# A decoder layer's first feed-forward product: three of eight pairs of tiles by seven products in eight of ten groups

## The chip, the cores and the metric

One core of one Trainium2 chip runs the whole kernel. The metric is device microseconds (us) of one execution; lower is better. Engines are named as in the profile: PE is TensorE's matmul row and PEld its weight loads, DVE is VectorE, ACT is ScalarE, POOL is GpSimd, SP is SyncE, whose queue issues the DMAs.

## The reference

One layer of a decoder for 256 tokens of width 2048 in float32: a token mixer (four mLSTM heads and eight dilated-attention heads), cross-attention into 256 memory tokens, and a SwiGLU channel mixer, each followed by `x <- LN(alpha * x + f(x))`. The change lies in the channel mixer:

```
def swiglu_ffn(x, w1, w3, w2):
    return (jax.nn.silu(x @ w1) * (x @ w3)) @ w2
```

with `x` 256 x 2048, `w1` and `w3` 2048 x 5632 and `w2` 5632 x 2048.

## The kernel before

**Numbers.** Every float32 operand is split into a high part (ACT casts it, L114) and a low part (DVE subtracts the high part from the operand, L115). A product is three matmuls, high by high, high by low and low by high, added up in PSUM.

**Groups and blocks.** The first feed-forward product is made in eleven groups of hidden features, `f0`, `f2`, ... `f20`; `f0` has code of its own, the ten others run in the loop at the end of `decoder_layer`. One group multiplies x2 (the layer's input at that point, 256 x 2048) by 1024 weight columns, 512 of `w1` and `w3` each. It walks over eight blocks of weights. A block is two 128-row tiles (a pair) by 1024 columns, 1 MB, fetched by SP in two DMAs of 512 KB (`fetch_pair`, L210) into one of RAW = 3 buffers, named `f18w` in group f18. The DMA for a block waits until DVE has read the last of the block that lay in that buffer.

**Plain blocks.** `plain` splits the two tiles (two casts and two subtractions of 128 x 1024) into `f18h` and `f18l`; there are SPLIT = 5 buffers for each. `tile_products` then issues 24 matmuls of 128 x 512 columns: 2 tiles x 2 token halves x 2 column halves x 3.

**Blocks by seven products.** A block in parentheses in `plan`, such as `(2,)`, is taken as a 2 x 2 product of quarter blocks, with seven products in place of eight, the Strassen-Winograd scheme: 21 matmuls. Three DVE instructions form the sums of weights: L292 (128 x 1024, into `f18t`), L296 and L297 (128 x 512 each, into `f18s`). Then four pieces are split, of 512, 1024, 1024 and 1024 columns. I call them P1, P23, P57 and Q64 after the products they serve; block 2's are 2.P23 and so on, and the two halves of a plain block 7 are 7a and 7b. The matching sums of x2 (`x2m`) are made once, by `mix_again`, and kept.

**Banks.** P2, P3, Q4 and E gather the plain blocks too. After the last block by seven, `early` (L679 to L683) empties the banks P1, P5, P7 and Q6 on DVE while plain blocks still run; `whole` (L691) adds the other four when the group ends. `hidden` then applies silu and the gate, transposes and splits the result into `hT`, and for the pairs listed in SEVENS also mixes it (L145 to L148, `hTm`). That work falls into the next group's time.

**What sets the order.** All of this part is ordered by the framework: it replays the program on a cost model of its own while it lays instructions out, so the order on each engine is fixed when the kernel is built, and so is the choice of buffers. At run time each engine takes its instructions in that order and waits on semaphores. An L292 that waits for its block's DMA therefore holds all that stands behind it on DVE.

The ten groups used `plan = [0, 1, (2,), 3, 4, (5,), 6, 7]`. In groups f2 and f4, DVE also applies the norm's gain and bias to z (`ln.rest`, L745), one instruction after each block. After f10, the first half of the second feed-forward product (`w2a0`, `w2a1`) runs, after f20 the rest (`w2b0`, `w2b1`).

**Memory.** On-chip working memory beside the pools is cut into NSLOT slots of 128 x 1024 float32 (4,096 bytes of each partition), handed out in turn by `big` and, in halves, `slot`.

Of the kernel before, what the change touches and what calls it, by code (L numbers as in the profile page):

```python
# [11 lines left out]
F32 = mybir.dt.float32  # L12
F32R = mybir.dt.float32r
# [6 lines left out]
P = 128  # L20
D = 2048
S = 256
KT = D // P
# [9 lines left out]
NEG = -1.0e30  # L33
U = 2 * S - 1
W = 1024
NSLOT, RAW, SPLIT = 34, 3, 5
LAG, HEAD, POOLED, LAG2 = 6, 8, 5, 8
WARM = 2

# [13 lines left out]
def decoder_layer(ctx: ExitStack, tc: tile.TileContext, A):  # L53
# [4 lines left out]
    const = ctx.enter_context(tc.tile_pool(name="const", bufs=1))  # L58
# [12 lines left out]
    def big(name, dt=F32R):  # L71
        i = free_slots.pop(0)
        t = up.tile([P, 1024], dt, tag=f"u{i}", name=name)
        held[id(t)] = (i, t)
        return t

    def slot(name):
        if len(free_halves) < 3 and free_slots:
            t = big(name, F32)
            i, _ = held.pop(id(t))  # L80
            pair = {"i": i, "free": 2}
            for c in range(2):
                free_halves.append((t[:, c * 512 : (c + 1) * 512], pair))
        t, pair = free_halves.pop(0)
        pair["free"] -= 1
        held[id(t)] = (pair, t)
        return t

    def free(*tiles):
        for t in tiles:  # L90
            where, _ = held.pop(id(t))
            if isinstance(where, int):
                free_slots.append(where)
                continue
            where["free"] += 1
            if where["free"] == 2:
                free_halves[:] = [x for x in free_halves if x[1] is not where]
                free_slots.append(where["i"])
            else:
                free_halves.append((t, where))  # L100
# [93 lines left out]
    def fetch(src, name):  # L194


        def get(b):
            w = wp.tile([P, 2, W], F32, tag="w", name=f"{name}w{b}", bufs=RAW)
            nc.sync.dma_start(out=w, in_=src[b])
            return w  # L200

        return get

    def fetch_pair(src, name):


        def get(b):
            w = wp.tile([P, 2, W], F32, tag="w", name=f"{name}w{b}", bufs=RAW)
            for c in range(2):
                nc.sync.dma_start(  # L210
                    out=w[:, :, c * 512 : (c + 1) * 512],
                    in_=src[c][b // 2][:, b % 2].rearrange("p (s c) -> p s c", s=2),
                )
            return w

        return get
# [454 lines left out]
    def into_rows(rows, name):  # L671


        def early(of):
            u = slot(f"{name}u")
            for m in range(2):
                rows.append([slot(f"{name}{m}{c}") for c in range(2)])
            (r11, r12), (r21, r22) = rows
            SC.copy(r11, of["P1"])  # L679
            V.tensor_tensor(out=u, in0=r11, in1=of["Q6"], op=ALU.subtract)  # L680
            V.tensor_tensor(out=r21, in0=u, in1=of["P7"], op=ALU.add)
            V.tensor_tensor(out=r12, in0=of["P5"], in1=u, op=ALU.subtract)
            V.tensor_tensor(out=r22, in0=r12, in1=of["P7"], op=ALU.subtract)  # L683
            free(u)

        return early

    def whole(rows, banks):
        for m in range(2):
            for c in range(2):  # L690
                V.tensor_tensor(out=rows[m][c], in0=rows[m][c], in1=banks[m][c], op=ALU.add)  # L691
# [100 lines left out]
    sel_t = slot("sel")  # L792
# [3 lines left out]
    nc.sync.dma_start(out=cw, in_=A["conv"])  # L796
    gb = const.tile([8, 1], F32, tag="gb", name="gb")
    nc.sync.dma_start(out=gb, in_=A["gate_b"])
    gw = const.tile([P, KT, 8], F32, tag="gw", name="gw")
    nc.sync.dma_start(out=gw, in_=A["w_gate"])  # L800

    gw2 = const.tile([P, KT, 40], F32R, tag="gw2", name="gw2")
    gz = slot("gwz")
    V.memset(gz, 0.0)
    V.tensor_copy(gw2[:, :, 8:32], gz.rearrange("p (k c) -> p k c", k=KT)[:, :, :24])
# [6 lines left out]
        attention(2 * j, qk0[j], qk0[2 + j], [va[m][0] for m in range(2)], tb)  # L812
    qk1 = in_features(2) + in_features(3)
    es, least_norm = gates()
    free(sel_t)
    for j in range(2):
        attention(4 + 2 * j, qk1[j], qk1[2 + j], [va[m][1] for m in range(2)], tb)
    free(*va[0], *va[1])
# [63 lines left out]
    for g in range(2):  # L882
        get, plan = fetch(A["w_out"][g], f"wo{g}"), [0, 2, (1,), 4, 5, (3,), 6, 7]
# [101 lines left out]
    plan = [0, 2, (1,), 4, (3,), 5, 6, 7]  # L985
# [3 lines left out]
    plan, kept = [0, (1,), 2, (3,), 4, 5, 6, 7], range(KT - LAG, KT)  # L989
# [115 lines left out]
    def hidden(j, banks, parts, name):  # L1105

        for i in range(2):
            hs = []
            for m in range(2):
                h = slot(f"{name}h{i}{m}")  # L1110
                g, u = parts(banks[m], i)
                SC.activation(h[:, :256], g, ACT.Silu)
                V.tensor_tensor(out=h[:, :256], in0=h[:, :256], in1=u, op=ALU.mult)
                hs.append(h)
            pt = sbank(f"{name}p{i}")
            for s in range(2):
                for m in range(2):
                    T.transpose(
                        pt[:, s * S + m * P : s * S + (m + 1) * P], hs[m][:, s * P : (s + 1) * P], ident
                    )  # L1120
            if j + i in SEVENS:
                h = slot(f"{name}t{i}")
                SC.copy(h, pt)
                hT.put(j + i, h)
                hT.mix(j + i, h)
                free(h)
            else:
                hT.put(j + i, pt)
            free(*hs)
# [4 lines left out]
    def w2_first():  # L1134
        plan = [0, 1, 3, (2,), 5, (4,), 7, (6,), 9, (8,), 10, 11]
        for c in range(2):
            banks = gemm_seven(
                hT, fetch(A["w2"][c][:half], f"w2a{c}"), 2 * half, f"w2a{c}", plan, into_z(c, ALPHA),
                last=c == 1,
            )  # L1140
            for m in range(2):
                add(m, c, banks, scale=1.0)

    for j in (2, 5):
        x2.mix_again(j)
    rest = ln.rest()
    for g in range(2, n, 2):
        get, rows = fetch_pair(A["w13"][g - 2 : g], f"f{g}"), []
        plan = [0, 1, (2,), 3, 4, (5,), 6, 7]
        between = (lambda: next(rest, None)) if g < half else None  # L1150
        banks = gemm_seven(x2, get, KT, f"f{g}", plan, into_rows(rows, f"f{g}r"), last=g == n - 2, between=between)
        whole(rows, banks)
        hidden(g, rows, lambda b, i: [b[i][:, x * 256 : (x + 1) * 256] for x in range(2)], f"f{g}")
        free(*rows[0], *rows[1])
        if g == half - 2:
            w2_first()
# [3 lines left out]
    plan = [0, (1,), 2, (3,), 4, (5,), 6, 7, 8, 9]  # L1160
# [3 lines left out]
    plan = [(1,), 0, (3,), 2, (5,), 4, 6, 7, 8, 9]  # L1164
# [107 lines left out]
```

## Time and profile before

| | us |
|---|---|
| runs of the kernel before | 1541.36, 1539.50, 1541.11 (median 1541.11) |
| the profiled execution | 1540.81 |
| its span, first to last instruction | 1539.0 |
| granted TensorE clock (mean) | 0.998 |

The profile shows one execution, whose own time is 1540.81 us; 1.8 us of that lie outside the span. Rows of the timeline give start, duration, engine, line, operation, out<-in and shape, and in brackets how long the engine had been idle and what ended that. A displayed duration on DVE and PE runs on into the next instruction of the same engine, so what an instruction costs its engine is the distance between two starts when nothing waits. Group f18 lies at 1335.8 to 1378.9 us.

### The profile page before, as it was taken

To read this page: it belongs to the slowest core of one execution; us is meant where nothing else is said; L and a number is where in the kernel's file an instruction comes from. 1 tells how busy PE (TensorE), PEld (TensorE's weight loads), DVE (VectorE), ACT (ScalarE), POOL (GpSimd) and SP (SyncE) were. 2 spreads that over 40 slices of the span, in tenths; PEclk is the share of its full clock that TensorE was granted. 3 is DMA by queue.
4 is the path that set the end of the run, shared out by engine and by line. 5 is a ranking of instruction groups with operands and counts; after the bars stand their busy time and mean duration, and the time that the engine had idled before them with its cause. 6 is when DMAs were issued, how large, how long until landed. Compare 5 with 4: busy or idle time off the path is not lost.

```text
span 1539.0 us, 19369 instructions
## 1 busy us (share of the span) xinstructions
PE 1522.7 (99%) x7394; PEld 1273.8 (83%) x7394; DVE 1233.4 (80%) x1663; ACT 797.0 (52%) x1054; POOL 9.3 (1%) x18
## 2 busy tenths in 40 slices
PE   9999999999999999999999999999999999999997
PEld 7888888888888878888888888887788888888885
DVE  7665788787799888657798788888788878888897
ACT  5444645554544555445557454555545455455551
POOL 0000000000000000000000000000000000000000
PEclk9999999999999999999999999999999999999999
DMA  8674445664654546445564555665455666567552
GB/s 303 208 272 165 140 172 210 232 237 160 232 191 172 205 171 221 162 165 179 177 218 165 174 182 192 218 195 200 156 215 208 200 192 194 192 205 260 197 186 109
DMA packets 83419, 301.37 MB, mean 196 GB/s; under 512 B 7213, under 2 KB 9466, under 8 KB 59774
## 3 DMA queue, kind: packets, MB, share of 16 engines
q1 hardware_dynamic: 83326, 300.14, 56.6%
q8 instruction: 58, 0.95, 0.2%
q14 instruction: 35, 0.29, 0.1%
HBM read 297.99 MB, written 4.21 MB: 196 GB/s over the span
## 4 chain that ended last, share of the span: by engine, by line
PE 95%; DVE 3%; DMA 1%; issue 0%; ACT 0%; DVEq 0%; SPq 0%; ACTq 0%
PE w2a1P L323 2%; PE w2a0P L323 2%; PE w2b0P L323 2%; PE w2b1P L323 2%; PE f10P L323 2%; PE v1P L323 2%; PE xo0P L323 2%; PE wo0P L323 2%; PE f4P L323 2%; PE f14P L323 2%; PE f6P L323 2%; PE f20P L323 2%; PE f16P L323 2%; PE f18P L323 2%; PE v0P L323 2%; PE wo1P L323 2%
## 5 line engine op out<-in xcount | busy, mean ns | idle before, releaser
L114 ACT CAST w2a1h<-w2a1w 128x1024 fp32r<-128x1024 f32 (+1 forms) x24 | 22.5, 980 | 23.3 <-PE w2a1E L323 14.5
L114 ACT CAST w2a0h<-w2a0w 128x1024 fp32r<-128x1024 f32 (+1 forms) x24 | 22.8, 980 | 17.8 <-PE w2a0E L323 10.7
L115 DVE TENSOR_TENSOR w2a0l<-w2a0w,w2a0h 128x1024 fp32r<-128x1024 f32 (+1 forms) x24 | 26.5, 1129 | 6.1 <-ACT w2a0h L114 6.1
L115 DVE TENSOR_TENSOR w2a1l<-w2a1w,w2a1h 128x1024 fp32r<-128x1024 f32 (+1 forms) x24 | 26.3, 1128 | 5.6 <-ACT w2a1h L114 5.6
L114 ACT CAST w2b0h<-w2b0w 128x1024 fp32r<-128x1024 f32 (+1 forms) x20 | 19.3, 987 | 17.3 <-PE w2b0E L323 9.8
L114 ACT CAST w2b1h<-w2b1w 128x512 fp32r<-128x512 f32 (+1 forms) x28 | 19.8, 758 | 12.9 <-PE w2b0E L323 5.4
L323 PE MATMUL w2a0P<-w2a0h,hT 128*128 128x512 f32 x80 | 26.2, 391 | 0.2 <-ACT w2a0h L114 0.2
L323 PE MATMUL w2a1P<-w2a1h,hT 128*128 128x512 f32 x80 | 25.4, 389 | 0.0
L114 ACT CAST wo1h<-wo1w 128x1024 fp32r<-128x1024 f32 (+1 forms) x16 | 15.6, 1001 | 18.9 <-PE wo1E L323 11.3
L264 PE MATMUL f0b<-f0h,x 128*128 128x512 f32 x64 | 25.4, 397 | 0.0
L114 ACT CAST f12h<-f12w 128x1024 fp32r<-128x1024 f32 (+1 forms) x16 | 15.6, 1000 | 18.7 <-PE f12E L323 9.9
L265 PE MATMUL f0b<-f0l,x 128*128 128x512 f32 x64 | 25.1, 392 | 0.1
L114 ACT CAST xv0h<-xv0w 128x1024 fp32r<-128x1024 f32 (+1 forms) x16 | 15.2, 970 | 18.5 <-PE xv0E L323 7.1
L115 DVE TENSOR_TENSOR w2b0l<-w2b0w,w2b0h 128x1024 fp32r<-128x1024 f32 (+1 forms) x20 | 22.2, 1137 | 3.0 <-ACT w2b0h L114 3.0
L115 DVE TENSOR_TENSOR v0l<-v0w,v0h 128x1024 fp32r<-128x1024 f32 (+1 forms) x16 | 18.2, 1154 | 7.8 <-ACT v0h L114 7.7
L115 DVE TENSOR_TENSOR xo0l<-xo0w,xo0h 128x1024 fp32r<-128x1024 f32 (+1 forms) x16 | 18.2, 1153 | 7.3 <-ACT xo0h L114 7.2
L114 ACT CAST v0h<-v0w 128x1024 fp32r<-128x1024 f32 (+1 forms) x16 | 15.7, 1000 | 16.0 <-PE v0E L323 9.9
L114 ACT CAST v2h<-v2w 128x1024 fp32r<-128x1024 f32 (+1 forms) x16 | 15.6, 1000 | 16.2 <-PE v2E L323 10.8
L115 DVE TENSOR_TENSOR w2b1l<-w2b1w,w2b1h 128x512 fp32r<-128x512 f32 (+1 forms) x28 | 22.7, 854 | 1.5 <-ACT w2b1h L114 1.5
L387 PE MATMUL i0b<-xT,i0h 128*128 128x512 f32 x64 | 22.6, 427 | 0.8 <-ACT i0h L114 0.8
L115 DVE TENSOR_TENSOR wo0l<-wo0w,wo0h 128x1024 fp32r<-128x1024 f32 (+1 forms) x16 | 18.2, 1153 | 6.4 <-ACT wo0h L114 6.4
L387 PE MATMUL xk1b<-mT,xk1h 128*128 128x512 f32 x64 | 23.0, 401 | 0.3 <-ACT xk1h L114 0.3
(1719 smaller groups left out, 5556.6 us busy)
## 6 DMA issues: line engine op xcount, KB each, us to landing
w2a0w<-in_w SPq DMA_DIRECT2D x12, 1024.0 KB, 4.8
w2a1w<-in_w SPq DMA_DIRECT2D x12, 1024.0 KB, 5.7
w2b0w<-in_w SPq DMA_DIRECT2D x10, 1024.0 KB, 4.9
w2b1w<-in_w SPq DMA_DIRECT2D x10, 1024.0 KB, 5.0
v0w<-in_w_v SPq DMA_DIRECT2D x8, 1024.0 KB, 5.1
v1w<-in_w_v SPq DMA_DIRECT2D x8, 1024.0 KB, 4.8
v2w<-in_w_v SPq DMA_DIRECT2D x8, 1024.0 KB, 4.8
wo0w<-in_w_out SPq DMA_DIRECT2D x8, 1024.0 KB, 4.9
```

The source lines that it names most:

```text
L114: SC.copy(hi, src)
L115: latest["lo"] = V.tensor_tensor(out=lo, in0=src, in1=as_f32(hi), op=ALU.subtract).ins
L264: T.matmul(banks[m][c], xh, wh[:, cs], start=n == 0, stop=False)
L265: T.matmul(banks[m][c], xh, wl[:, cs], start=False, stop=False)
L323: T.matmul(of[to], lhsT, rhs, start=to not in begun, stop=end)
L387: T.matmul(banks[f], wh[:, cs], op.both(kt), start=kt == 0, stop=end, skip_group_check=True)
```

## The change

The eight groups f6 to f20 take three blocks by seven products, (2,), (4,) and (6,), in place of two, (2,) and (5,), and in another order. Groups f2 and f4 keep two, now (2,) and (4,), in the order 0, 1, 3, (2,), 5, (4,), 6, 7. x2 is mixed for the pairs 2, 4 and 6 in place of 2 and 5; the third kept `x2m` needs a slot, so NSLOT is 35, and the two gate weights `gw` and `gw2`, which had memory of their own for the whole program, live in slots until the gates are made.

```
-NSLOT, RAW, SPLIT = 34, 3, 5
+NSLOT, RAW, SPLIT = 35, 3, 5
...
-    gw = const.tile([P, KT, 8], F32, tag="gw", name="gw")
+    gw_t, gw2_t = slot("gw"), big("gw2")
+    gw = gw_t[:, : KT * 8].rearrange("p (k c) -> p k c", k=KT)
...
-    gw2 = const.tile([P, KT, 40], F32R, tag="gw2", name="gw2")
+    gw2 = gw2_t[:, : KT * 40].rearrange("p (k c) -> p k c", k=KT)
...
-    free(sel_t)
+    free(sel_t, gw_t, gw2_t)
...
-    for j in (2, 5):
+    for j in (2, 4, 6):
         x2.mix_again(j)
...
-        plan = [0, 1, (2,), 3, 4, (5,), 6, 7]
+        plan = [0, 1, 3, (2,), 5, (4,), 6, 7] if g < 6 else [0, 1, (2,), 3, (4,), 5, (6,), 7]
```

One line is added ahead of L800, so L1113 of before is L1114 in the change.

DVE at the end of group f16, before, from the second half of block 7 of f16 (`f16l_11286`) to the second L691; `f18l` are the subtractions of f18's blocks 0 and 1, L292 is the first sum of its block (2,):

```order
L115 TENSOR_TENSOR f16l_11286<-f16w_11266,f16h_11285 128x1024
L681 TENSOR_TENSOR f16ru<-f14t_10973,f16P_10991 128x512
L682 TENSOR_TENSOR f16ru<-f16P_10990,f14t_10973 128x512
L115 TENSOR_TENSOR f18l_11351<-f18w_11347,f18h_11350 128x1024
L683 TENSOR_TENSOR f16r_11224<-f16ru,f16P_10991 128x512
L115 TENSOR_TENSOR f18l_11367<-f18w_11347,f18h_11366 128x1024
L292 TENSOR_TENSOR f18t_11420<-f18w_11417 128x1024
L115 TENSOR_TENSOR f18l_11386<-f18w_11382,f18h_11385 128x1024
L296 TENSOR_TENSOR f18s_11421<-f18t_11420,f18w_11417 128x512
L691 TENSOR_TENSOR f14t_10973<-f14t_10973,f16P_10985 128x512
```

The same place in the change, from `f16l_11350`, the second half of block 7:

```order
L115 TENSOR_TENSOR f16l_11350<-f16w_11330,f16h_11349 128x1024
L115 TENSOR_TENSOR f18l_11415<-f18w_11411,f18h_11414 128x1024
L680 TENSOR_TENSOR f14t_11027<-f14t_11027,f16Q_11046 128x512
L115 TENSOR_TENSOR f18l_11431<-f18w_11411,f18h_11430 128x1024
L115 TENSOR_TENSOR f18l_11450<-f18w_11446,f18h_11449 128x1024
L681 TENSOR_TENSOR f16ru<-f14t_11027,f16P_11045 128x512
L682 TENSOR_TENSOR f16ru<-f16P_11044,f14t_11027 128x512
L292 TENSOR_TENSOR f18t_11484<-f18w_11481 128x1024
L115 TENSOR_TENSOR f18l_11466<-f18w_11446,f18h_11465 128x1024
L691 TENSOR_TENSOR f14t_11027<-f14t_11027,f16P_11039 128x512
```

L292 has moved behind a third subtraction (three of the four halves of blocks 0 and 1 now stand ahead of it), and `early` begins (L680) behind the last subtraction of its group rather than ahead of it.

DVE in the middle of group f18, before, around its second and last L292 (of block (5,)); `f18l_11482` is the second half of block 3, `f18l_11501` and `f18l_11517` are block 4:

```order
L115 TENSOR_TENSOR f18l_11482<-f18w_11462,f18h_11481 128x1024
L292 TENSOR_TENSOR f18t_11535<-f18w_11532 128x1024
L115 TENSOR_TENSOR f18l_11501<-f18w_11497,f18h_11500 128x1024
L145 TENSOR_TENSOR f16h_11317<-f16h_11317 128x128
L146 TENSOR_TENSOR f16h_11317<-f16h_11317 128x128
L115 TENSOR_TENSOR hT_11329<-f16h_11317,hT_11329 128x2x256
L115 TENSOR_TENSOR f18l_11517<-f18w_11497,f18h_11516 128x1024
L296 TENSOR_TENSOR f18s_11536<-f18t_11535,f18w_11532 128x512
```

The same group in the change, around its third L292 (of block (6,)); `f18l_11577`, `f18l_11587` and `f18l_11597` are 4.P23, 4.P57 and 4.Q64, `f18l_11610` is the first half of block 5:

```order
L115 TENSOR_TENSOR f18l_11577<-f18w_11561,f18h_11576 128x1024
L145 TENSOR_TENSOR f16h_11381<-f16h_11381 128x128
L146 TENSOR_TENSOR f16h_11381<-f16h_11381 128x128
L147 TENSOR_TENSOR f16h_11381<-f16h_11381 128x128
L115 TENSOR_TENSOR hT_11393<-f16h_11381,hT_11393 128x2x256
L148 TENSOR_TENSOR f16h_11381<-f16h_11381 128x128
L115 TENSOR_TENSOR f18l_11587<-f18t_11564,f18h_11586 128x1024
L292 TENSOR_TENSOR f18t_11644<-f18w_11641 128x1024
L115 TENSOR_TENSOR f18l_11597<-f18s_11565,f18h_11596 128x1024
L115 TENSOR_TENSOR hTm_11400<-f16h_11381,hTm_11400 128x512
L296 TENSOR_TENSOR f18s_11645<-f18t_11644,f18w_11641 128x512
L115 TENSOR_TENSOR f18l_11610<-f18w_11606,f18h_11609 128x1024
```

L292 of block (6,) now stands in the midst of block (4,)'s splits: 4.Q64 and both halves of block 5 come behind it. The buffer of block (6,)'s weights is the one that block 3 held, so its DMA waits for the second half of block 3 on DVE.

## The prediction

> **What bounds the kernel now.** I read the page first: busy time and the chain of waits.
>
> ```profile
> PE 1522.7 (99%) x7394; PEld 1273.8 (83%) x7394; DVE 1233.4 (80%) x1663; ACT 797.0 (52%) x1054; POOL 9.3 (1%) x18
> PE 95%; DVE 3%; DMA 1%; issue 0%; ACT 0%; DVEq 0%; SPq 0%; ACTq 0%
> ```
>
> PE carries 95% of the chain. A displayed matmul is longer than what it costs, so I checked with the chain's own merged rows and the windows of three groups (columns: window, its length, then busy time and count of PE, PEld, DVE, ACT):
>
> ```profile
> 1336.14 5.44 PE f18P L323 x24
> 1249.50:1292.60 43.10, 43.10 (x195) 35.59 (x194) 34.94 (x46) 23.65 (x29) 0.00 (x0) 1.00 0.60 194
> 1292.60:1335.80 43.20, 43.20 (x196) 35.67 (x195) 36.47 (x46) 23.67 (x29) 0.00 (x0) 1.00 0.61 196
> 1335.80:1378.90 43.10, 43.10 (x196) 35.59 (x195) 34.85 (x46) 23.66 (x29) 0.00 (x0) 1.00 0.62 193
> ```
>
> One matmul costs 5.44 / 24 = 0.2267 us. A group has 6 x 24 + 2 x 21 = 186 of them, 42.17 us; eight small transposes take the other 0.93 of 43.10. Nothing is left for waiting: in these groups PE sets the time. DVE is busy 34.9 to 36.5 us of each 43.1, ACT 23.7. So matmuls taken away shorten the group, as long as DVE keeps up.
>
> **Where a low share of waiting can mislead.** DVE takes its instructions in a fixed order, and an L292 that waits for its weights holds all behind it. The timeline of DVE shows how long such a reload takes: from the start of the subtraction that frees the buffer to the start of the L292 that needs the new weights.
>
> ```profile
> 1258.84 1.22 DVE L115 TENSOR_TENSOR f14l<-f14w,f14h 128x1024 fp32r<-128x1024 f32 x1 [2.60 <-ACT f14h L114]
> 1265.91 1.23 DVE L292 TENSOR_TENSOR f14t<-f14w 128x1024 f32<-128x1024 f32 x1 [0.38 <-DMA f14w<-in_w]
> ...
> 1325.97 1.22 DVE L115 TENSOR_TENSOR f16l<-f16w,f16h 128x1024 fp32r<-128x1024 f32 x1
> 1333.61 1.22 DVE L292 TENSOR_TENSOR f18t<-f18w 128x1024 f32<-128x1024 f32 x1 [2.35 <-DMA f18w<-in_w]
> ...
> 1345.13 1.23 DVE L115 TENSOR_TENSOR f18l<-f18w,f18h 128x1024 fp32r<-128x1024 f32 x1 [2.83 <-ACT f18h L114]
> 1352.34 1.23 DVE L292 TENSOR_TENSOR f18t<-f18w 128x1024 f32<-128x1024 f32 x1 [0.51 <-DMA f18w<-in_w]
> ...
> 1369.12 1.22 DVE L115 TENSOR_TENSOR f18l<-f18w,f18h 128x1024 fp32r<-128x1024 f32 x1
> 1377.44 1.22 DVE L292 TENSOR_TENSOR f20t<-f20w 128x1024 f32<-128x1024 f32 x1 [3.04 <-DMA f20w<-in_w]
> ```
>
> In each pair DVE waited for the weights alone at the end, so the distance is the reload: 7.07 and 7.21 us in the middle of a group (f14, f18), 7.64 and 8.32 across a group's end (into f18, f20). Today PE has cover for each. That such a wait can reach PE is seen in xv0, an earlier product with the same order and three blocks by seven, and PE also stalled once in f10:
>
> ```profile
> 547.05 1.23 DVE L292 TENSOR_TENSOR xv0t<-xv0w 128x1024 f32<-128x1024 f32 x1 [3.17 <-DMA xv0w<-in_xv]
> PE xv0P L323 <- DVE xv0l L115: 0.5, 2, 0.3
> 1051.17 0.50 PE L323 MATMUL f10Q<-f10h,x2m 128*128 128x512 f32 x1 [0.34 <-ACT f10h L114]
> ```
>
> **The change, part by part.** *PE.* Each group of the eight has one block of 21 matmuls in place of one of 24. That removes 8 x 3 = 24 matmuls of 128 x 512, by chance as many as the x24 row above: 5.44 us. A group falls from 43.10 to 183 x 0.2267 + 0.93 = 42.42 us.
>
> *DVE.* Costs are distances between starts:
>
> ```profile
> 1291.29 1.23 DVE L292 TENSOR_TENSOR f16t<-f16w 128x1024 f32<-128x1024 f32 x1 [3.18 <-DMA f16w<-in_w]
> 1292.44 1.22 DVE L115 TENSOR_TENSOR f16l<-f16w,f16h 128x1024 fp32r<-128x1024 f32 x1
> 1293.57 0.68 DVE L296 TENSOR_TENSOR f16s<-f16t,f16w 128x512 f32<-128x512 f32 x1
> ...
> 1347.41 0.42 DVE L1113 TENSOR_TENSOR f16r<-f16r 128x256 f32<-128x256 f32 x1
> 1347.75 0.68 DVE L115 TENSOR_TENSOR hT<-f16p,hT 128x512 fp32r<-128x512 f32 x1
> 1348.35 1.21 DVE L115 TENSOR_TENSOR f18l<-f18s,f18h 128x1024 fp32r<-128x1024 f32 x1
> ...
> 1354.62 0.28 DVE L145 TENSOR_TENSOR f16h<-f16h 128x128 f32<-128x128 f32 x1
> 1354.82 0.28 DVE L146 TENSOR_TENSOR f16h<-f16h 128x128 f32<-128x128 f32 x1
> ```
>
> So 1.14 us for 1024 columns, 0.60 for 512, 0.34 for 256, 0.20 for 128. A plain block costs 2 x 1.14 = 2.28 on DVE; one by seven costs its splits 0.60 + 3 x 1.14 = 4.02 and its sums 1.14 + 2 x 0.60 = 2.34, in all 6.36: 4.08 us more per group. A full group now has 22 instructions of 1024, 20 of 512, 4 of 256 and 4 of 128: 25.1 + 12.0 + 1.4 + 0.8 = 39.3 us, where before it had 35.2 (the windows say 34.9 to 36.5). That fits into 42.42, with 3.1 to spare.
>
> *The loop.* But those 3.1 us must hold the waits for three reloads, and in the new order each holds back splits that PE soon needs. What DVE does inside each reload, by its order in the change (the first and the third are shown above): across the group's end, the freeing subtraction, three more and L680 to L682, 4 x 1.14 + 3 x 0.60 = 6.4 us; behind block 1, for (4,): the subtraction, four L691, L683, L296, L297, 2.P1 and two gate products (L1114), 1.14 + 8 x 0.60 + 2 x 0.34 = 6.6; behind block 3, for (6,): the subtraction, 4.P1, 4.P23, 4.P57, L145 to L148 and hT, 3 x 1.14 + 2 x 0.60 + 0.8 = 5.4. Together 18.4, so 39.3 - 18.4 = 20.9 us lie outside. A group cannot be shorter than 20.9 plus three reloads (each at least what is done inside it). PE sets the time while the three sum to under 42.42 - 20.9 = 21.5, a mean of 7.17 us. With 7.64 across the end and 7.07 and 7.21 inside they sum to 21.92: 0.4 us over. Splits run ahead of PE by up to five buffers, so some of this is absorbed; I take 0.3 us per group, between nothing (three of 7.07) and 3.5 (three of 8.32). It concerns the six groups with full work, f6, f8, f10, f14, f16 and f18: 1.8 us (0 to 21). In f12 no `hidden` falls, and f20 has no mixing, which leaves DVE 1.4 us or more.
>
> *The end of f20.* There the eight 256 KB rows of the last norm are loaded between the blocks, and a reload took longer:
>
> ```profile
> 1388.27 1.23 DVE L115 TENSOR_TENSOR f20l<-f20w,f20h 128x1024 fp32r<-128x1024 f32 x1 [2.13 <-ACT f20h L114]
> 1397.39 1.23 DVE L292 TENSOR_TENSOR f20t<-f20w 128x1024 f32<-128x1024 f32 x1 [2.42 <-DMA f20w<-in_w]
> ```
>
> 9.12 us, 2 above 7.07. Block (6,)'s DMA now stands behind four of those loads in SP's queue, and w2b0 opens with a block by seven soon after. I charge 1.0 us, once (0 to 2.5: all of the 2 us and a little at the seam, or hidden by the lead).
>
> *The rest, at nothing.* ACT gains 1,536 columns of cast a group, about 1.6 us on 23.7 of 43.1. The third mixing of x2 (0.60 + 4 x 0.20 + 0.60 = 2.0 us of DVE) falls into f2, whose other order changes no count:
>
> ```profile
> 862.80:905.90 43.10, 43.10 (x196) 35.72 (x195) 34.99 (x43) 22.37 (x28) 0.00 (x0) 1.00 0.58 191
> 153.90:192.40 38.50, 38.50 (x220) 32.72 (x219) 30.10 (x57) 23.74 (x43) 0.00 (x0) 1.00 0.40 140
> ```
>
> DVE has 8.1 us idle there. The move of `gw` and `gw2` shifts which slot every tile gets, and with it the order of attention, gates and mLSTM; in that stretch (second row) PE has 38.50 of 38.50 busy and DVE 8.4 free, so I expect no change, within 1 us either way.
>
> **The sum.** 1540.81 - 5.44 + 1.8 + 1.0 = 1538.2 us against the profiled execution, which lies 0.3 below the median of 1541.11. About 0.2%, 3.1 us, is what a measurement of this kernel can tell from no change, so faster means under 1538.0: the forecast stands on the edge.
>
> **The rivals.**
>
> *Full cover.* The lead of five buffers takes in all reload waits, or undisturbed they take 7.1: all 5.44 us stay, 1535.4. For it: w2a0 and w2a1 alternate four blocks by seven with plain ones, and PE was idle 0.86 us in the 127.9:
>
> ```profile
> 1079.40:1207.30 127.90, 127.04 (x562) 104.13 (x562) 105.67 (x118) 64.83 (x72) 0.00 (x0) 1.00 0.56 197
> ```
>
> Against it: they have no `hidden`, and DVE was busy 83% of that window, where a group of the change needs 39.3 of 42.42, 93%.
>
> *The loop sets the pace at no gain.* If the reloads average 7.5 (between 7.21 and 7.64), a group takes 20.9 + 22.5 = 43.4, 1.0 over PE's 42.42: six groups give back 6.0, f20 1.0, so 1542.4 - about what it was.
>
> *Slower: the reload across the end is the rule.* If all three take 7.64 or more, the group takes 43.8 or more, 1.4 over: 8.4 + 1.0 given back, 1544.8; at 8.32, 20.9 + 25.0 = 45.9, and 1557. It decides at 7.6 us. For it: the two reloads measured across a group's end; against: those inside.
>
> *Slower: DVE instructions don't overlap.* At displayed length (1.22, 0.68, 0.42, 0.28) DVE's work is 26.8 + 13.6 + 1.7 + 1.1 = 43.2 us without any wait, 0.8 over PE; with 2 us of reload waits six groups give back 17 us: 1553. The starts at 1291.29, 1292.44 and 1293.57, each before the displayed end of the one ahead, speak against it. The Trainium skill ("VectorE: DVE Perf Modes", section "The DRAIN you can't avoid") has such a rule: the next instruction does not start until the pipe has emptied; it also allows that one which is not held starts earlier, and these rows agree with that.
>
> **How the numbers follow.** Forecast 0.45, its own range 1536.4 to 1540 (0 to 0.6 us per group), half of it on either side of 1538.0; full cover 0.22; no gain 0.18; slower by reloads 0.12; slower by DVE 0.03. Faster: 0.22 + 0.22 = 0.44. Same: 0.23 + 0.17 = 0.40. Slower: 0.16. The range runs from 1535.0 (full cover, and f10's stall of 0.34 gone too) to 1544.5, which leaves out the slower cases.
>
> **What would show it.** Right: groups f6 to f18 at 42.4 to 43.0 us, three L292 waits per group on DMA of 0.5 to 2 us, DVE above 38 busy, and short PE waits in these groups for low parts of 4.Q64 and block 5. Wrong: groups over 43.3 (the loop), or no PE wait at all (full cover); or a stretch before f2 whose length differs by over 1 us, which this sum does not have.

## The result and the profile after

The change made the kernel slower. Four runs took 1563.49, 1562.11, 1560.53 and 1563.95 us, median 1562.8; the kernel before, beside them, 1540.86. The ratio is 1.0142, with a 95% interval of 1.0124 to 1.016: 21.9 us. The profiled execution took 1563.49 us, its span 1560.0 (before: 1540.81 and 1539.0). The page of the change, busy time and chain:

```profile
PE 1526.8 (98%) x7370; PEld 1272.4 (82%) x7370; DVE 1270.6 (81%) x1709; ACT 809.5 (52%) x1071; POOL 10.4 (1%) x18
PE 91%; DVE 5%; DMA 2%; ACT 1%; issue 1%; SPq 0%; DVEq 0%; ACTq 0%
```

PE has 24 matmuls fewer and carries 91% of the chain, where it carried 95%. The list of PE's waits (total, times, longest) tells where it stood still:

```profile
PE f10Q L323 <- ACT f10h L114: 3.7, 1, 3.7
PE w2b0P L323 <- DVE w2b0l L115: 2.9, 2, 2.6
PE pt L497 <- DVE xTr L493: 2.5, 1, 2.5
PE pt L497 <- DVE g L493: 2.4, 1, 2.4
PE pt L497 <- DVE apT L493: 1.9, 1, 1.9
...
PE w2a0P L323 <- DVE w2a0l L115: 1.6, 1, 1.6
```

Three of these lie in attention, 700 us ahead of the product that was changed, and three at the ends of its two halves: f10, w2a0 and w2b0. To see what each place cost I took from the trace the start of each product's first matmul, and from two neighbours the length between them (differences taken before rounding):

| stretch | before | change | difference |
|---|---|---|---|
| start to f2 | 863.1 | 874.4 | +11.4 |
| f2 to f8 | 172.4 | 169.2 | -3.1 |
| f10 | 44.3 | 49.5 | +5.3 |
| w2a0 | 65.3 | 70.1 | +4.8 |
| w2a1 | 62.6 | 62.6 | 0 |
| f12 to f18 | 171.6 | 168.1 | -3.5 |
| f20 and w2b0 | 97.0 | 103.2 | +6.1 |
| w2b1 to the end | 62.9 | 62.9 | 0 |

In the change a group with three blocks leaves its last eight matmuls, 8 x 0.2267 = 1.8 us, behind the first matmul of what follows. With that taken out, and against a length without the matmuls removed, f10 lost 49.5 - (44.3 - 0.68) = 5.9 us, w2a0 4.8 - 1.8 = 3.0, f20 and w2b0 6.1 - 1.8 + 0.7 = 5.0, the stretch ahead of f2 11.4. The eight groups save 5.4, and 1.1 is spread over the rest, 0.7 of it in f16: 11.4 + 5.9 + 3.0 + 5.0 - 5.4 + 1.1 = 21.0, the difference of the spans.

**The middle groups do what was forecast.** Windows of f14, f16 and f18 (length, then busy time and count of PE, PEld, DVE, ACT):

```profile
1265.90:1308.30 42.40, 42.40 (x192) 35.01 (x191) 39.27 (x51) 24.73 (x32) 0.00 (x0) 1.00 0.59 194
1308.30:1351.40 43.10, 42.80 (x192) 35.00 (x192) 40.25 (x51) 25.16 (x32) 0.00 (x0) 1.00 0.60 201
1351.40:1393.90 42.50, 42.50 (x192) 35.05 (x191) 39.34 (x51) 24.77 (x32) 0.00 (x0) 1.00 0.59 193
```

42.4 to 42.5 us where PE alone needs 42.42, DVE at 39.3 as counted. The reloads in f18, each from the subtraction that frees the buffer to the L292 (DVE's timeline; the last freeing subtraction is the first of the two in its row):

```profile
1346.01 1.23 DVE L115 TENSOR_TENSOR f16l<-f16w,f16h 128x1024 fp32r<-128x1024 f32 x1 [0.21 <-ACT f16h L114]
1352.73 1.23 DVE L292 TENSOR_TENSOR f18t<-f18w 128x1024 f32<-128x1024 f32 x1 [0.29 <-DMA f18w<-in_w]
1353.87 1.22 DVE L115 TENSOR_TENSOR f18l<-f18w,f18h 128x1024 fp32r<-128x1024 f32 x1
...
1361.01 1.23 DVE L292 TENSOR_TENSOR f18t<-f18w 128x1024 f32<-128x1024 f32 x1 [0.46 <-DMA f18w<-in_w]
...
1369.30 1.81 DVE L115 TENSOR_TENSOR f18l<-f18w,f18h 128x1024 fp32r<-128x1024 f32 x2
...
1376.04 1.23 DVE L292 TENSOR_TENSOR f18t<-f18w 128x1024 f32<-128x1024 f32 x1
```

6.72, 7.14 and 6.74 us, mean 6.87, under the break-even of 7.17. The third L292 did not wait at all (its row shows no idle time), so that reload took 6.74 us at most.

**Ahead of f2.** PE, DVE and the DMA queue in the two windows where it was lost, before and then after (the last three columns are PE's granted clock, the DMA share and GB/s):

```profile
133.00:141.00 8.00, 8.00 (x49) 7.01 (x47) 7.19 (x11) 5.83 (x9) 0.00 (x0) 1.00 0.50 170
196.00:203.00 7.00, 7.00 (x44) 6.13 (x43) 6.38 (x12) 4.64 (x11) 0.00 (x0) 1.00 0.43 150
```

```profile
133.00:141.00 8.00, 5.47 (x32) 4.36 (x31) 1.89 (x6) 2.07 (x7) 0.00 (x0) 0.86 0.00 0
196.00:203.00 7.00, 2.58 (x14) 1.95 (x14) 3.63 (x11) 2.41 (x8) 0.00 (x0) 1.00 0.00 1
```

After, every engine is idle for much of the time and nothing is being loaded. No engine is short of time; they wait for each other in a ring. DVE's timeline of the change shows the ring:

```profile
135.53 0.56 DVE L482 SCALAR_TENSOR_TENSOR xTr<-sc,tb 128x384 f32<-128x384 f32 x1 [8.71 <-PE sc L480]
...
144.02 0.76 DVE L403 TENSOR_TENSOR v0r<-i2b,xTr 128x256 f32<-128x256 f32 x2 [5.67 <-PE po L503]
...
146.65 3.50 DVE L115 TENSOR_TENSOR i3l<-i3w,i3h 128x1024 fp32r<-128x1024 f32 x3 [1.17 <-ACT i3h L114]
...
196.48 0.43 DVE L838 TENSOR_SCALAR v1r<-v1r 128x512 f32<-128x512 f32 x1 [1.52 <-DMA v1r<-in_mh_g]
...
204.39 0.78 DVE L403 TENSOR_TENSOR me<-i4b,g 128x256 f32<-128x256 f32 x2 [2.33 <-PE po L503]
```

L403 empties two banks of product i2 into a piece of working memory (`v0r`), and that piece is one that an attention head still reads: it has to wait for the head's last product (`po`). The splits of i3 (`i3l`) stand behind it, and the DMA of the next weights waits for those splits. So DVE waits for PE, PE for the head that DVE still works on, and the queue for both. The same happens again at 204.39 with i4 and i5. At 196.48 a row of `mh_g` takes part: its load stands in SP's queue ahead of v1's weights and waited 9.2 us for the product that still read its half slot.

```profile
SPq L837 <- PE po L504: 9.2, 1, 9.2
```

**f10.** Here DVE had time to spare: it stood idle for 3.42 us until 1056.27 and was busy from there on. PE's wait of 3.67 us at 1065.01 ends with the cast of 2.Q64, and that needs the sums L296 and L297 of block (2,). The first L292 below is that of block (2,), the second already that of block (4,):

```profile
1045.55 1.23 DVE L292 TENSOR_TENSOR f10t<-f10w 128x1024 f32<-128x1024 f32 x1 [0.70 <-DMA f10w<-in_w]
...
1056.27 1.23 DVE L115 TENSOR_TENSOR f10l<-f10w,f10h 128x1024 fp32r<-128x1024 f32 x1 [3.42 <-ACT f10h L114]
...
1058.54 1.22 DVE L292 TENSOR_TENSOR f10t<-f10w 128x1024 f32<-128x1024 f32 x1
...
1061.60 0.29 DVE L148 TENSOR_TENSOR f8ru<-f8r,f8ru 128x128 f32<-128x128 f32 x1
1061.93 0.69 DVE L296 TENSOR_TENSOR f10s<-f10t,f10w 128x512 f32<-128x512 f32 x1
```

In f18 L296 of block (2,) stands 4 us behind its L292, at 1356.80. In f10 it comes 16.4 us behind, after L145 to L148 of f8's `hidden`. By the order it waits for L148, the last to read that piece of `f8r`: `f10s` was given the memory of one of f8's rows. The splits of blocks 2 and 3 and the weights of what follows wait with it.

### The profile page after: what moved, and what is told of

It is laid out like the page before. It is cut to its first block, busy times and chain, and to the rows that moved or that the text cites. A ratio compares the mean times of both kernels' runs of the same rounds, so it can differ in the third digit from the quotient of the medians.

```text
span 1560.0 us, 19388 instructions
## 1 busy us (share of the span) xinstructions
PE 1526.8 (98%) x7370; PEld 1272.4 (82%) x7370; DVE 1270.6 (81%) x1709; ACT 809.5 (52%) x1071; POOL 10.4 (1%) x18
## 4 chain that ended last, share of the span: by engine, by line
PE 91%; DVE 5%; DMA 2%; ACT 1%; issue 1%; SPq 0%; DVEq 0%; ACTq 0%
PE w2a1P L323 2%; PE w2a0P L323 2%; PE w2b1P L323 2%; PE w2b0P L323 2%; PE xv1P L323 2%; PE f12P L323 2%; PE xv0P L323 2%; PE f6P L323 2%; PE xo0P L323 1%; PE v1P L323 1%; PE v0P L323 1%; PE wo0P L323 1%; PE wo1P L323 1%; PE v2P L323 1%; PE f2P L323 1%; PE xo1P L323 1%
## 5 line engine op out<-in xcount | busy, mean ns | idle before, releaser
L114 ACT CAST w2a0h<-w2a0w 128x1024 fp32r<-128x1024 f32 (+1 forms) x24 | 22.4, 979 | 15.2 <-PE w2a0E L323 10.2
L114 ACT CAST f12h<-f12w 128x1024 fp32r<-128x1024 f32 (+1 forms) x16 | 15.2, 972 | 19.7 <-PE f12E L323 11.5
L115 DVE TENSOR_TENSOR f2l<-f2w,f2h 128x1024 fp32r<-128x1024 f32 (+1 forms) x16 | 18.3, 1155 | 6.7 <-ACT f2h L114 6.6
L115 DVE TENSOR_TENSOR v2l<-v2w,v2h 128x1024 fp32r<-128x1024 f32 (+1 forms) x16 | 18.2, 1154 | 6.6 <-ACT v2h L114 6.6
L114 ACT CAST f4h<-f4w 128x1024 fp32r<-128x1024 f32 (+1 forms) x16 | 15.8, 1000 | 15.0 <-PE f4E L323 8.1
L323 PE MATMUL w2b0P<-w2b0h,hT 128*128 128x512 f32 x68 | 23.1, 392 | 0.0
```

The source lines that it names most:

```text
L114: SC.copy(hi, src)
L115: latest["lo"] = V.tensor_tensor(out=lo, in0=src, in1=as_f32(hi), op=ALU.subtract).ins
L323: T.matmul(of[to], lhsT, rhs, start=to not in begun, stop=end)
```

## The experiments

All twelve, in a table first; the last four columns are from the profiled execution of each, the ratios to runs of the kernel before on the same chip. "Lost" is a stretch's length over what its matmuls need, 43.1 us for a group with two blocks by seven and 42.4 with three, without the eight matmuls that fall across a border; for f20 with w2b0 it is the difference from before.

| run | time | ratio to before (95%) | f2 starts | lost in f10 | w2a0 | f20, w2b0 |
|---|---|---|---|---|---|---|
| before | 1540.86 | | 863.1 | 1.2 | 65.3 | 0 |
| change | 1562.80 | 1.0142 (1.0124 to 1.016) | 874.4 | 7.1 | 68.3 | 5.0 |
| e1 | 1549.38 | 1.0053 (1.0036 to 1.007) | 874.7 | 0.0 | 63.6 | 0.8 |
| e2 | 1553.89 | 1.0084 (1.0069 to 1.0099) | 863.6 | 10.0 | 67.6 | 6.5 |
| e3 | 1547.55 | 1.0049 (1.0034 to 1.0064) | 863.3 | 4.3 | 67.3 | 5.9 |
| e4 | 1549.28 | 1.0058 (1.0043 to 1.0073) | 862.5 | 8.0 | 65.3 | 6.1 |
| e5 | 1539.98 | 1.0000 (0.9991 to 1.0009) | 863.6 | 4.6 | 65.3 | 0.3 |
| e6 | 1551.02 | 1.0073 (1.0058 to 1.0089) | 863.1 | 7.5 | 67.7 | 3.3 |
| e7 | 1537.33 | 0.9984 (0.9975 to 0.9993) | 862.6 | 0.0 | 63.6 | 0.2 |
| e8 | 1539.03 | 0.9991 (0.9982 to 1.0000) | 860.5 | 4.5 | 65.3 | -0.1 |
| e9 | 1554.88 | 1.0096 (1.0082 to 1.0109) | 877.4 | 1.2 | 65.3 | -0.4 |
| e10 | 1550.26 | 1.0065 (1.0051 to 1.0079) | 860.1 | 7.9 | 69.8 | 5.7 |
| e11 | 1540.84 | 1.0004 (0.9995 to 1.0013) | 864.1 | 1.2 | 65.3 | -0.5 |
| e12 | 1533.85 | 0.9959 (0.9946 to 0.9973) | 860.6 | 0.0 | 63.6 | 0.0 |

**e1 and e2: the two parts of the change.** e1 is the kernel before with the first four pieces of the diff (NSLOT 35, `gw` and `gw2` in slots until the gates), and nothing else.

> The kernel before with the move of the two gate weights and NSLOT 35 alone; plans and mixings as before. Theory (slots): the loss of 11.4 us ahead of group f2 comes from this move alone. Until the gates are made it takes 1.5 slots and gives 1, so results of i2 and the row of mh_g wait for slots that attention still holds, and DVE has splits queued behind them. f2 then starts at about 874 us and the time is 1540.9 + 11.4 = 1552. Rival (product): the time was lost in the feed-forward groups, and the early shift has little to do with this edit: f2 at 863 and about 1541.

e2 is the change with this edit:

```
-    free_slots = list(range(NSLOT))
+    free_slots = list(range(NSLOT - 1))
...
-    gw_t, gw2_t = slot("gw"), big("gw2")
-    gw = gw_t[:, : KT * 8].rearrange("p (k c) -> p k c", k=KT)
+    gw2_t = up.tile([P, 1024], F32R, tag=f"u{NSLOT - 1}", name="gw2")
+    gw = const.tile([P, KT, 8], F32, tag="gw", name="gw")
...
-    free(sel_t, gw_t, gw2_t)
+    free(sel_t)
...
+    free_slots.append(NSLOT - 1)
     for j in (2, 4, 6):
```

> The change with the early stretch of before: gw has its own memory again, and gw2 lies in the 35th slot, which is handed out only just ahead of the mixings of x2, so that the order up to f0 is that of before. Theory (slots and seams): the groups gain 5.4 us and lose about 6.0 in f10, 3.0 at the start of w2a0 and 5.0 in f20 and w2b0: f2 at 863 us and 1540.9 + 9.6 = 1550.5. Rival (the prediction's sum): without the early disorder the product is worth what was forecast, about 1538.

Each part alone costs time, 8.5 us and 13.0 against 21.9 together. In e1 f2 starts at 874.7, as in the change: the early loss is the move of the gate weights. In e2 it starts at 863.6, and f10, w2a0, f20 and w2b0 lose about what they lost in the change, but f10 3 us more, which put e2 3.4 us over its expectation. The 3 us are a reload across the group's end: from the freeing subtraction (1027.55) to f10's first L292 (1036.93) it took 9.38 us, where the change took 7.13, and PE waited 2.3 us for the low part behind it. In e6, which lays out the same order up to there, it took 8.50 us and PE waited 1.4. So a reload differs from one execution to the next, and one of 8.5 us does reach PE. The rival of e2, the sum as forecast, would have been 1538. e1 was 2.6 us faster than expected, and that is news: f10 and w2a0 are 1.2 and 1.7 us shorter than before. From here on e1's extra slot is a suspect of its own.

**e3 and e4: why f10 stalls.** Both are e2 with another order in f10:

```
+        if g == 10:
+            plan = [0, 1, 3, (2,), (4,), 5, (6,), 7]
```

```
+        if g == 10:
+            plan = [0, 1, (2,), 3, (4,), 5, 6, 7]
```

> e2 with the order 0, 1, 3, (2,), (4,), 5, (6,), 7 in f10 alone: still three blocks by seven, but block (2,) one block later. Theory (slots): f10's stall of 3.7 us comes from L296 of block (2,), which must wait for a slot that hidden of f8 holds; a block later that slot is free in time, and 4 to 6 us of f10's 6.0 come back: 1545 to 1546.5. Rival (load): three blocks by seven are too much for DVE in f10: 1550 or more.

> e2 with the order 0, 1, (2,), 3, (4,), 5, 6, 7 in f10 alone: only two blocks by seven there, the first two where the change has them. Theory (slots): the stall stays, since the same two blocks want slots at the same time, and three matmuls more are issued: 1550.5 + 0.7 = 1551. Rival (load): with 4.1 us less on DVE the stall goes: about 1545.

With one block by seven less, and 4.1 us less on DVE, f10 still stalls (e4); with all three, but the first a block later, more than half of the loss goes (e3). PE's waits in e4, then in e3:

```profile
PE f10Q L323 <- ACT f10h L114: 3.7, 1, 3.7
```

```profile
PE f10Q L323 <- ACT f10h L114: 1.8, 1, 1.8
```

So it is not DVE's load in f10. Neither expectation was met quite: e3 ended 1 us above its range, and e4, at 1549.28, between its theory (1551) and its rival (1545). In e3 the slot is not free in time, either: L296 of block (2,) still comes 15.2 us behind its L292. The block is only needed later. w2a0 falls back to 65.3 in e4 and stays at 67.3 in e3: its 3 us go with the third block in f10. That is shown; how the one leads to the other I did not follow.

**e5 and e6: the ends.** e5 is e2 with the plan of f2 and f4, `[0, 1, 3, (2,), 5, (4,), 6, 7]`, in f10 and f20. e6 is e2 with one line moved:

```
-    ln = Norm(2, "l2")
...
     banks = gemm_seven(hT, fetch(A["w2"][0][half:], "w2b0"), nkt, "w2b0", plan, into_z(0, 1.0), order)
+    ln = Norm(2, "l2")
```

> e2 with the order 0, 1, 3, (2,), 5, (4,), 6, 7 (two blocks by seven, late) in f10 and f20; f6, f8, f12, f14, f16 and f18 keep three. Theory (slots and seams): what e2 lost lay in f10, at the start of w2a0, in f20 and in w2b0 alone, and goes but for about 1.5 us; the six groups keep 0.65 each: 1540.9 - 3.9 + 1.5 = 1538.5. Rival (load): DVE's lag is carried from the six groups into the ends, whatever plan these have: 1545 or more.

> e2 with the eight rows of the last norm loaded after w2b0's first blocks and no more in f20. Theory (rows): in f20 block (6,)'s weights took 6.9 us to land because the rows were moved at the same time; without them L292 is not late, w2b0's first block by seven isn't either, and 4 to 6 us of the 7.6 lost in f20 and w2b0 come back: 1548 to 1550. Rival (load): f20 is late because of its third block by seven alone, and nothing comes back: 1553.

e5 confirms that the six middle groups carry nothing into the ends: f20 and w2b0 lose 0.3. But f10 still lost 4.6 us with two late blocks, so e5 came to 1539.98, 1.5 over the expectation, and no better than before. e6 brought back 3.2 of the 6.5 us in f20 and w2b0, less than the 4 to 6 expected: the rows of the norm are half of that loss, and the third block itself the other half (e5, without it, lost 0.3). DVE's L292 of f20's block (6,) and of w2b0's first, in e2 and then in e6:

```profile
1412.07 1.23 DVE L292 TENSOR_TENSOR f20t<-f20w 128x1024 f32<-128x1024 f32 x1 [3.31 <-DMA f20w<-in_w]
1426.36 1.23 DVE L292 TENSOR_TENSOR w2b0t<-w2b0w 128x1024 f32<-128x1024 f32 x1 [2.91 <-DMA w2b0w<-in_w]
```

```profile
1407.41 1.23 DVE L292 TENSOR_TENSOR f20t<-f20w 128x1024 f32<-128x1024 f32 x1 [1.46 <-DMA f20w<-in_w]
1422.62 1.22 DVE L292 TENSOR_TENSOR w2b0t<-w2b0w 128x1024 f32<-128x1024 f32 x1 [1.60 <-DMA w2b0w<-in_w]
```

Both waits are halved with the rows gone: the loop of DVE and DMA that the prediction described, with the larger part of its price in w2b0, whose first block by seven inherits the lateness.

**e7 and e11: is it a slot?** e7 is the kernel before with e2's 35th slot, plans and mixings as before; e11 is e7 with one word more, `for j in (2, 5, 7)`, a third pair of x2 mixed, kept and never used.

> The kernel before with nothing but the 35th slot, handed out just ahead of the mixings of x2 (until then gw2 lies in it); plans and mixings as before. Theory (slots): f10's short stall and the one at the start of w2a0 come from a missing slot, as in e1, where they were gone and the two stretches were 2.9 us shorter: 1538. Rival (rotation): e1's gain there came from another order after its early part, and one slot more changes nothing: 1541.

> e7 with a third pair of x2 (7) mixed and kept, which no product uses: old plans, 35 slots, one of them held. Theory (slots): f10 and the start of w2a0 fall back to the 44.3 and 65.3 us of before, 2.9 us, for want of that slot: 1537.3 + 2.9 = 1540.2. Rival: the mixing costs nothing and e7's gain stays: 1537.3.

Windows of f10 in e7, then in e11, and between them the first two sums of block (2,) in e7:

```profile
1034.90:1078.00 43.10, 43.10 (x195) 35.67 (x194) 36.06 (x47) 23.76 (x30) 0.00 (x0) 1.00 0.58 196
```

```profile
1033.89 1.23 DVE L292 TENSOR_TENSOR f10t<-f10w 128x1024 f32<-128x1024 f32 x1 [1.89 <-DMA f10w<-in_w]
1035.15 0.69 DVE L296 TENSOR_TENSOR f10s<-f10t,f10w 128x512 f32<-128x512 f32 x1
```

```profile
1036.50:1080.80 44.30, 43.74 (x196) 35.55 (x195) 35.97 (x47) 23.84 (x30) 0.00 (x0) 1.00 0.58 194
```

One free slot takes all waiting out of f10, one slot held puts it back, and both times came within 0.7 us of the theory. In e7 L296 of block (2,) stands directly behind L292, 1.26 us, as in e1 and e12, where f10 loses nothing. In all other runs, before and the change among them, it comes 14.2 to 18.0 us behind. f10 and w2a0 were short of a slot before the change already, for 2.9 us; the third kept pair uses up the added slot. That the plan with early blocks (2,) and (4,) wants room for the sums of two blocks at once, while f8's rows still hold theirs, and that this makes the loss larger than before, is argued: no run gives that plan one slot more. e7 is faster than both kernels.

**e9 and e10: what disorders the early stretch.** The first guess behind e1's expectation was the number of slots that are missing until the gates. The order of the instructions spoke against it: a whole slot held left it nearly as before, half of one did not. e9 is the kernel before with this, e10 the change with that:

```
+    gw_t = slot("gw")
     gw = const.tile([P, KT, 8], F32, tag="gw", name="gw")
...
-    free(sel_t)
+    free(sel_t, gw_t)
```

```
-    gw_t, gw2_t = slot("gw"), big("gw2")
+    gw_t, gw2_t = big("gw", F32), big("gw2")
```

> The kernel before with one half slot taken where the change takes gw's and given back after the gates, unused; the weights keep their own memory, 34 slots, old plans. The order shows the early disorder of the change with this alone, and none with a whole slot held in the same way. Theory (the half): half a slot held breaks up the recycling of halves, so that results of i2 get halves that attention still reads; f2 at about 874.5 and 1540.5 + 11.5 = 1552. Rival (count): what counts is how many slots are missing, and half of one is not felt: 1541.

> The change with one word altered: gw takes a whole slot in place of half of one, so that two slots rather than one and a half are missing until the gates. Theory (the half): the early disorder goes, f2 at 860 to 864, and the time is that of e2 or 2 to 3 us less: 1550 to 1554. Rival (count): with fewer slots the early stretch is as slow as in the change or slower: 1562 or more.

DVE's timeline, e9 and then e10 (`i3l` is what PE and the queue waited for in the change; before, the result of i2 went to `i2t` at 128.25, as in e10):

```profile
134.22 0.56 DVE L482 SCALAR_TENSOR_TENSOR xTr<-sc,tb 128x384 f32<-128x384 f32 x1 [8.72 <-PE sc L480]
142.69 0.76 DVE L403 TENSOR_TENSOR v0r<-i2b,xTr 128x256 f32<-128x256 f32 x2 [5.66 <-PE po L503]
```

```profile
128.14 0.42 DVE L403 TENSOR_TENSOR i2t<-i2b,xTd 128x256 f32<-128x256 f32 x1 [0.23 <-ACT xTd L402]
132.71 0.56 DVE L482 SCALAR_TENSOR_TENSOR apT<-sc,tb 128x384 f32<-128x384 f32 x1 [4.15 <-PE sc L480]
134.43 1.23 DVE L115 TENSOR_TENSOR i3l<-i3w,i3h 128x1024 fp32r<-128x1024 f32 x1 [0.51 <-ACT i3h L114]
```

2 KB per partition held and never used cost 14.7 us (1554.88 against 1540.16 for the runs of before beside it); taking 2 KB more, so that the gate weights hold two whole slots, took 12.5 us off the change. The ring needs only the half. `slot` hands out halves and takes a new whole slot only while fewer than three halves are at hand; that a held half keeps its partner in this small circle, so that the next results get the halves freed last, is argued from the code. That the half is the cause, and that i2 is then given memory which attention reads, is shown. e9 ended 2.9 us over its expectation; it lacks the 3 us that e1, with the 35th slot, gets back between xv0 and xo0.

**e8 and e12: a better version.** In e8, which is e5 otherwise, and in e12 the 35th slot is handed out when mLSTM ends. e12 keeps the old plan in f2 to f10 and in f20, and mixes pair 7 only behind w2a1:

```
-        plan = [0, 1, (2,), 3, 4, (5,), 6, 7]
+        plan = [0, 1, (2,), 3, (5,), 4, (7,), 6] if half <= g < n - 2 else [0, 1, (2,), 3, 4, (5,), 6, 7]
...
             w2_first()
+            x2.mix_again(7)
```

> e5 with the 35th slot handed out already at the end of mLSTM (about 340 us) rather than ahead of the mixings. Theory (slots): xv0, xv1 and xo0 were shorter by 6.3 us in e1, xq3 longer by 2.7, with one slot more; if that was the slot, 3 us come back here: about 1535. Rival (rotation): those differences came with the other order of e1's early part: 1538.5, as e5.

> e7 with the 35th slot handed out at the end of mLSTM as in e8, and three blocks by seven, (2,), (5,) and (7,) in the order 0, 1, (2,), 3, (5,), 4, (7,), 6, in f12, f14, f16 and f18 alone; the third pair is mixed only after w2a1, when the first half of the hidden features has given its slots back. f20 keeps the plan of before. Theory: 1537.3 - 2.6 (early slot) - 2.0 (four groups at 0.3 to 0.65) = 1533. Rival (load): the groups with three blocks push their lag into f20 and w2b0, which lose 3 to 5 us as in e2: 1537.

In both f2 starts 2.5 us earlier, from xv0, xv1 and xo0, as in e1: that gain is the slot's and not the reordering's. e8's time moved by 0.95 us against e5, where about 3 were expected; f10 still loses 4.5. e12 has no stall left of those in the list above: its four groups with three blocks gain 0.7, 0.3, 0.1 and 0.7, f20 and w2b0 lose nothing. 1533.85 us, 6.3 under the runs of before beside it and 29 under the change.

## Why the prediction was wrong

- **Matmuls removed, DVE's work, the loop: right.** 42.4 to 42.5 us in f8, f14 and f18, DVE 39.3 busy. In these groups the rival of full cover held: reloads of 6.9 us on average left no stall where 0.3 us was charged; f16 alone lost 0.7. Only at f10's start did a reload across the end reach PE, in e2, e4, e6 and e10 (9.38, 8.15, 8.50 and 8.10 us; PE waited 2.3, 1.1, 1.4 and 1.0).
- **"The rest, at nothing": the step that failed.** The move of `gw` and `gw2` was charged nothing, "within 1 us either way", because PE was full and DVE had 8.4 us free in that stretch. It cost 11.4 us. Free time of an engine says nothing here: what counts is which memory an instruction is given, whom it then waits for, and what stands behind it. The order is fixed when the kernel is built, and in it `v0r` was already the target of i2's result, ahead of the splits of i3; the prediction judged the stretch by busy shares alone, in a window (153.9 to 192.4) that lies between the two places where the time was lost. Its last sign of being wrong, a stretch before f2 off by over 1 us, came.
- **f10: counted as one of six like groups.** Its row of 0.34 us was quoted as a sign that a reload wait can reach PE. It was no reload wait. It was a wait for a slot, as e7 and e11 show. Under the new plan L296 waits in the same way and f10 loses 7.1 us; w2a0's 3.0 hang on f10's third block (e4). None of the rivals had a term for memory.
- **The end of f20: right mechanism, wrong size.** The slow reload beside the norm's rows was forecast at 1.0 us (0 to 2.5). It cost 5.0, 6.5 in e2, since w2b0 opens with a block by seven and its own L292 came 2.9 us late in turn; the rows are half of it (e6).
- **Stalls were priced at their length.** PE came back from some of them at half speed (last section): behind f10's 3.7 us, 13 matmuls from 1065.01 to 1070.75 took 5.7 us in place of 2.9. With the stall itself that is 6.5 of the 7.1 us.
- **The range** reached to 1544.5. Its slower rivals were priced from reloads alone; the time was 18 us outside. 11.4 + 5.9 + 3.0 + 5.0 = 25.3 us were lost in places for which the sum had 0.3 and 1.0.

## What to carry to other kernels

When a change moves a buffer into a shared pool, look in the order, not in the busy shares, for each instruction whose target is now a piece that something else still reads, and ask what stands behind it; here half a slot held unused cost 14.7 us, and one slot more gained 3.0. Before adding work to a loop, look for the iteration at which the most memory is held: here the added work stood still where there had been a small stall before (0.34 us in f10). The Trainium skill ("Perfetto Trace Analysis", section "Optimization Strategy") says that a gap which repeats on the engine that should be full can mean that memory for the next tile is missing; the trace agrees as to the cause (e7 against e11), though here the gap was a single one.

## What the hardware showed that was not expected

PE is slower for some microseconds after some stalls. PE's timeline of the change behind the wait at 138.49 (2.53 us) and behind f10's (3.67 us):

```profile
139.07 0.41 PE L515 MATMUL pgate<-xT,gw 128*8 128x256 f32 x1
139.29 0.41 PE L514 MATMUL pgate<-xT,gw 128*40 128x256 f32 x1
...
142.26 0.28 PE L514 MATMUL pgate<-xT,gw 128*40 128x256 f32 x1
142.38 0.28 PE L515 MATMUL pgate<-xT,gw 128*8 128x256 f32 x1
...
1065.01 0.79 PE L323 MATMUL f10Q<-f10h,x2m 128*128 128x512 f32 x1 [3.67 <-ACT f10h L114]
...
1067.40 0.63 PE L323 MATMUL f10Q<-f10l,x2m 128*128 128x512 f32 x1
1067.83 0.63 PE L323 MATMUL f10Q<-f10h,x2m 128*128 128x512 f32 x1
...
1071.21 0.39 PE L323 MATMUL f10Q<-f10l,x 128*128 128x512 f32 x1
1071.44 0.39 PE L323 MATMUL f10E<-f10l,x 128*128 128x512 f32 x1
```

Starts lie 0.22 us apart and then 0.12, and 0.43 and then 0.23: half speed until about 142.2 and 1070.7. Windows of the same trace give the granted clock (the third column from the end):

```profile
1065.00:1067.00 2.00, 1.99 (x5) 1.35 (x6) 2.00 (x3) 2.00 (x3) 0.00 (x0) 0.50 0.81 247
...
1071.00:1073.00 2.00, 2.00 (x10) 1.67 (x9) 0.65 (x1) 0.68 (x1) 0.00 (x0) 1.00 1.03 284
...
1444.40:1446.00 1.60, 1.60 (x6) 1.15 (x7) 1.60 (x3) 0.84 (x2) 0.00 (x0) 1.00 0.72 205
```

In e3, behind the stall of 2.56 us at the same place, which ends at 1428.87:

```profile
1431.00:1433.00 2.00, 2.00 (x6) 1.52 (x6) 2.00 (x3) 0.00 (x0) 0.00 (x0) 0.50 0.98 414
```

In the change the stall of 2.56 us in w2b0, which ends at 1444.40, was followed by full speed (last row of the change), the shorter one of 2.53 by half; in e3 a stall of the same 2.56 us was followed by half speed. So the length of a stall alone does not decide. The Trainium skill ("TensorE: Matmul & The Clock Gate", section "Part 1: The HAM clock gate (the "warmup" mystery)") has the clock halved after an idle window of about 3.4 us, and the window running freely. The half clock agrees with such a gate. The length does not: these stalls were shorter than 3.4 us or, in f10, the granted clock fell to 0.50 about 2.5 us after PE had stopped. That equal stalls end both ways would fit a window that runs freely; how much of it must be idle, no run here shows.
